# Two-layer diffusion trunk on one core: a written TensorE order for the second layer's experts

## The chip, the cores and the metric

The kernel runs on one core of a Trainium2 chip. The metric is device time in microseconds for one execution; the median of three executions stands for the kernel.

## The reference

The program computes two layers over 256 latent and 256 context tokens of width 1024: attention in four head groups, then a mixture of 16 SwiGLU experts of which each token takes two. The change lies in the experts of the second layer, which are computed for the 256 latent tokens alone:

```python
expert, w = route(hf, router_w, router_b)      # two experts of one group per token, weights sum to 1
xb = hf[buf_t].reshape(n_blocks, MOE_BLOCK, shp[-1])
def expert_block(args):
    xe, e = args
    return (jax.nn.silu(xe @ w_gate[e]) * (xe @ w_up[e])) @ w_down[e]
yb = lax.map(expert_block, (xb, blk_e)).reshape(P, shp[-1])
y = jnp.zeros_like(hf).at[buf_t].add(yb * buf_w[:, None].astype(yb.dtype))
x = x + m_lat[5] * y
```

`w_gate` and `w_up` are 1024 by 512 and `w_down` is 512 by 1024 for each expert, all fp32: six pieces of 1 MB for an expert, 96 for the layer.

## The kernel before

**The stage.** Class `MoeOnChip` computes the second layer's experts, 64 token slots for each. Tokens are neither gathered from nor scattered to DRAM. They are selected and put back by matmuls with 0/1 matrices, and the result is accumulated in four PSUM banks over all 16 experts.

**Names, with the lines of before.** `batch` (from L1253) builds for four experts at a time the 0/1 matrices `OH` on VectorE (L1259) and selects the tokens with them: 32 matmuls in four groups of eight (L1269), each group into one bank called `tr`. ScalarE (L1232) and VectorE (L1230) then bring the bank to `xTb`, each one half of it. `weights` (from L1279) multiplies `OH` with the table `tw` (a token's number and its weight) in eight fp32 matmuls (L1284), which gives each slot its token and weight, `sw`. `first` (from L995) does gate and up of one expert in two halves (L1007); a pair of its matmuls, one for gate and one for up, works on two halves of the array's columns. `hidden` is SiLU (ScalarE L1032), product (VectorE L1033), four transposes (TensorE L1037, bank `tr`) and a copy to `hT` (ScalarE L1046). `second` is w_down, in two halves (L1060, bank `S`). `store` scales the result by weight and gate (VectorE L1311, tile `selm`), splits it in two fp32r parts in `ys` (ScalarE L1314, VectorE L1315), and appends to the list `todo` the four matmuls that add the rows to the four accumulators (`add`, L1320; banks `ada`, `o`, `S`, `tr`).

Since four of the eight banks hold the accumulators, each of the tags `tr` and `S` has one bank left, and `mm` has two.

**Loops.** `experts` (from L1323) goes through e = 0 to 15. Round e issues `first` of expert e+1 with `hidden` of e between its halves, at e = 2, 6 and 10 the `batch` for the next four experts, then the pending `add`, then `second` of e, and at those three rounds `weights`.

**What sets the order.** A scheduler places the instructions of each engine; the code's order is where it starts from, and it may interleave the pieces above. `tc.issue_after` holds an instruction behind another; `tc.keep_in_program_order` keeps the instructions so marked in the order in which the code issues them. Weights come through SyncE's queue (L121) in the order in which they are used, each into a free slot of some 20 of 1 MB; `done_w` frees a slot when its matmuls are done.

Of the kernel before, what the change touches and what calls it, by code (L numbers as in the profile page):

```python
# [25 lines left out]
NE = 16  # L26
# [26 lines left out]
def body(tc, a, dbg=None):  # L53
# [18 lines left out]
    def psum(tag):  # L72
        return ps.tile([128, 512], F32, name=tag, bufs=dict(mm=2, ada=1, tr=2, S=2, o=1)[tag])


# [701 lines left out]

    class Moe:
        def __init__(self, l, tiles, pers, scr):
            self.l, self.tiles, self.scr = l, tiles, scr  # L780
# [215 lines left out]
        def first(self, e, between=None):  # L996
# [32 lines left out]
        def hidden(self, pa, pb):  # L1029
# [6 lines left out]
            for k in range(4):  # L1036
                PE.transpose(pt[:, k], h[:, 128 * k:128 * k + 128], ident[0:64, 0:64])  # L1037
            if pb is not None:
# [10 lines left out]
        def second(self, e):  # L1049
# [3 lines left out]
            for hf in range(2):  # L1053
                wd = next_w(f"e{l}")
                for g in range(2):
                    f = 2 * hf + g
                    for c in range(self.tiles_m):
                        m = 128 // self.tiles_m
                        t, h = c % (64 // m), 512 * (m * c // 64)
                        PE.matmul(py[m * c:m * c + m], lhsT=hT[:, f, m * t:m * t + m], rhs=wd[:, g, h:h + 512],  # L1060
                                  start=f == 0, stop=f == 3)
                if py2 is not None:
# [46 lines left out]
        def next(self, e, p):  # L1109
            def between():  # L1110
                self.hidden(*p)
                self.fetch(e + 2)
            if e + 1 < NE:
                return self.first(e + 1, between)
            self.hidden(*p)

        def overflow(self):
# [87 lines left out]

    class MoeOnChip(Moe):
        def persistent(self, pers):
            self.tw = pers.tile([128, self.nt, NE, 2], F32, name="tw")
            self.ms = pers.tile([128, self.nt, NE], F32, name="ms")
            self.cnt = pers.tile([128, NE], F32, name="cnt")  # L1210
            self.wsum = pers.tile([128, self.nt], F32, name="wsum")
            self.h2s = {}
# [22 lines left out]
        def tables(self, oh, M, pp):  # L1235
            nt, scr, tw = self.nt, self.scr, self.tw
            n16 = 16 * nt
            ms, wsum = self.ms, self.wsum
            for t in range(nt):
                G.tensor_scalar(tw[:, t, :, 0], iot[:, 0:16], 0.0, C["tok"][:, t:t + 1], op0=OP.mult, op1=OP.add)  # L1240

            V.tensor_mul(ms, M, self.score)
            V.tensor_copy(self.cnt, pp[:, n16:n16 + 16])
# [10 lines left out]
        def batch(self, e0):  # L1254
            p2, nt, n = self.p2, self.nt, 4
            OH = []
            for t in range(nt):
# [3 lines left out]
                                op=OP.is_equal)  # L1261
                OH.append(o)
            xT = p2.tile([128, 8, 64 * n], F32, name="xTb")
            for dp in range(4):
                px = psum("tr").rearrange("p (d n) -> p d n", d=2)
                for j in range(2):
                    d = 2 * dp + j
                    for i in range(2 * nt):
                        mm = PE.matmul(px[:, j].rearrange("p (e x) -> p e x", x=64),  # L1269
                                       lhsT=self.h2s[i % nt][i // nt][:, 128 * d:128 * d + 128],  # L1270
                                       rhs=OH[i % nt][:, :, 0], start=i == 0, stop=i == 2 * nt - 1)
# [4 lines left out]
            self.OH, self.last = OH, mm.ins  # L1276
# [26 lines left out]
        def store(self, e, py, py2):  # L1303
# [13 lines left out]
            def add():  # L1317
                for t in range(nt):
                    for c in range(2):
                        PE.matmul(self.acc[t, c], lhsT=oT[:, t], rhs=ys[:, c], start=False, stop=e == NE - 1)  # L1320
            self.todo.append(add)

        def experts(self, p2):  # L1323
            self.p2, self.xt = p2, {}
            self.sw, self.todo = {}, []

            self.sgh, self.y = scr2.rearrange("p a k n -> p (a k n)"), C["sel"].rearrange("p a n -> p (a n)")
            self.batch(0)
# [4 lines left out]
            with tc.issue_after(self.last):  # L1333
                for (t, c), acc in self.acc.items():
                    PE.matmul(acc, lhsT=ident, rhs=X[t][:, 512 * c:512 * c + 512], start=True, stop=False)
            self.rest()
            self.weights(0)
            add_tile("x", xx.rearrange("p t n -> p (t n)"))
            for e in range(NE):
                q = self.next(e, p)  # L1340
                if e % 4 == 2 and e + 2 < NE:
                    self.batch(e + 2)
                while self.todo and q:
                    self.todo.pop(0)()
                self.second(e)
                if e % 4 == 2 and e + 2 < NE:
                    self.weights(e + 2)
                p = q
            while self.todo:
                self.todo.pop(0)()  # L1350

# [15 lines left out]
        def overflow(self):  # L1367
# [3 lines left out]
            with tc.If(v > CAP):  # L1371
                ecol = p2.tile([128, 1], F32, name="ecol")
                V.memset(ecol, 0.0)
                with tc.For_i(0, NE, 1) as ei:
# [5 lines left out]
                    pos = p2.tile([128, nt, 2], F32, name="pos")  # L1380
                    for k, src in enumerate((self.posm, self.tw[:, :, :, 1])):
                        V.tensor_mul(pe_, src, eqb)
                        V.tensor_reduce(pos[:, :, k], pe_, axis=AX.X, op=OP.add)
                    for b in range(-(-(128 * nt - CAP) // 128)):
# [258 lines left out]
```

## Time and profile before

| what | value |
|---|---|
| median of 3 runs | 1273.6 us (1273.07 to 1274.47) |
| the profiled execution's own time | 1278.25 us |
| its span, first to last instruction | 1276.3 us |
| mean granted TensorE clock | 0.961 of full speed |
| busy share of the span: TensorE, VectorE, ScalarE, GpSimd | 91%, 45%, 33%, 19% |

The rows below are of this one execution, and times in them count from the start of its span. The experts of the second layer fill its last fifth, from about 1009 us on. TensorE's weight loads (PEld) overlap its matmuls. An fp32 matmul shows as two instructions, one of fp32r as one.

### The profile page before, as it was taken

The page shows a single profiled execution, that of the slowest core. Times are in us where ns is not written, and L with a number is a line of the kernel's source. Part 1 is how long each engine was busy: PE and PEld are TensorE (multiplying, and loading weights), DVE is VectorE, ACT ScalarE, POOL GpSimd, SP SyncE. Part 2 cuts the span into 40 slices and gives each one's busy share as a digit, 9 for nine tenths or more (in the row PEclk, how much of TensorE's full clock was granted, in tenths as well). Part 3 has the DMA queues.
Part 4 walks back from the last instruction along what each step waited for, and adds up shares of the span by engine and source line. Part 5 has one row for each costly group of instructions (what it writes and reads, how often), then busy time and mean ns, then how long its engine had stood idle before and what let it go on. Part 6 is the DMA issues. An engine that isn't in the chain of part 4 may idle for free.

```text
span 1276.3 us, 21459 instructions
## 1 busy us (share of the span) xinstructions
PE 1161.8 (91%) x8527; PEld 674.5 (53%) x8527; DVE 568.0 (45%) x1539; ACT 417.6 (33%) x1003; POOL 241.9 (19%) x268
## 2 busy tenths in 40 slices
PE   4999999999999589999999957989999699999996
PEld 2676667666645344444444426978875334333332
DVE  4556656565334742132222238785763523222222
ACT  3445445455133311111111115755542312111111
POOL 1231121221112612121121125341311200000000
PEclk9999899999999879999999988998999899999998
DMA  9746445454734569999999754223129799999940
GB/s 300 261 174 232 166 166 187 168 196 137 286 156 175 221 203 353 380 356 369 359 375 378 272 196 163 67 67 109 51 99 353 265 388 394 394 394 394 394 177 34
DMA packets 134639, 312.99 MB, mean 245 GB/s; under 512 B 7212, under 2 KB 38448, under 8 KB 129408
## 3 DMA queue, kind: packets, MB, share of 16 engines
q1 hardware_dynamic: 127936, 294.19, 63.6%
q0 software_dynamic: 3840, 8.40, 2.1%
q10 hardware_dynamic: 2752, 8.91, 1.9%
q8 instruction: 71, 1.16, 0.4%
q14 instruction: 40, 0.33, 0.1%
HBM read 305.11 MB, written 10.55 MB: 247 GB/s over the span
## 4 chain that ended last, share of the span: by engine, by line
PE 59%; DVE 7%; DMA 4%; issue 1%; ACT 1%; POOL 1%; ACTq 0%; SPq 0%; DVEq 0%; POOLq 0%
PE mm L1007 19%; PE S L1060 9%; PE mm L765 5%; PE mm L465 3%; PE o L1012 2%; PE ada L1012 2%; PE S L1066 2%; PE o L712 2%; PE ada L465 2%; PE tr L1269 2%; PE tr L644 1%; PE S L636 1%; PE tr L983 1%; DMA gb<-amd 1%; PE tr L1037 1%
## 5 line engine op out<-in xcount | busy, mean ns | idle before, releaser
L465 PE MATMUL mm<-ws,hT 128*128 128x256 f32 x1488 | 229.9, 296 | 5.4 <-DVE hT L504 1.8
L465 PEld LDWEIGHTS mm<-ws,hT 128*128 128x128 f32 x1488 | 200.8, 195 | 43.1 <-issue 25.1
L1007 PE MATMUL mm<-wb,xT 128*32 128x512 f32 x912 | 141.0, 607 | 0.0
L295 POOL TENSOR_TENSOR hss<-hss,mhalf 128x4 f32<-128x4 f32 (+2 forms) x56 | 66.9, 1196 | 186.6 <-DVE hss L294 170.8
L671 ACT ACTIVATE p<-S,nm 128x512 f32<-128x512 f32 (+1 forms) x120 | 73.7, 616 | 68.4 <-DVE nm L661 41.8
L661 DVE TENSOR_REDUCE nm<-S 128x1 f32<-128x512 f32 (+1 forms) x120 | 70.6, 596 | 26.5 <-PE S L636 22.4
L1060 PE MATMUL S<-wb,hT 128*32 128x512 f32 (+1 forms) x360 | 72.8, 595 | 0.0
L765 PE MATMUL mm<-wa,t4k 128*128 128x512 f32 x144 | 70.9, 615 | 0.0
L1007 PE MATMUL mm<-wb,xTb 128*64 128x512 f32 x240 | 69.6, 623 | 0.0
L974 POOL DMA_INDIRECT yd<-y,idx x32 | 36.9, 1152 | 165.4 <-DVE y L1085 160.6
L314 PE MATMUL ada<-wa,sc 128*32 128x512 f32 x320 | 63.1, 617 | 0.0
L1007 PEld LDWEIGHTS mm<-wb,xT 128*32 128x32 f32 x912 | 34.2, 111 | 49.0 <-issue 44.7
L644 PE MATMUL tr<-ident,p 128*128 128x128 f32 x320 | 51.0, 277 | 4.7 <-ACT p L671 4.4
L1046 ACT ACTIVATE hT<-tr 128x384 f32<-128x384 f32 (+1 forms) x32 | 14.0, 438 | 125.7 <-PE tr L1043 75.1
L452 ACT ACTIVATE ws<-wa 128x512 fp32r<-128x512 f32 x80 | 48.8, 630 | 18.7 <-PE mm L465 7.5
L712 PE MATMUL o<-PT,v 128*64 128x256 f32 x320 | 54.5, 390 | 0.1
L1060 PE MATMUL S<-wa,hT 128*32 128x512 f32 (+1 forms) x312 | 53.2, 593 | 0.6 <-ACT hT L1046 0.6
L454 POOL TENSOR_TENSOR ws<-wa,ws 128x512 fp32r<-128x512 f32 x20 | 27.7, 1387 | 136.5 <-ACT ws L452 110.7
L611 PE MATMUL tr<-identr,sk 128*128 128x128 f32 x312 | 47.6, 254 | 4.8 <-DVE sk L608 2.9
L1007 PE MATMUL mm<-wc,xTb 128*64 128x512 f32 x144 | 52.0, 597 | 0.0
L644 PEld LDWEIGHTS tr<-ident,p 128*128 128x128 f32 x320 | 36.4, 141 | 23.1 <-ACT p L671 11.6
L1033 DVE TENSOR_TENSOR sc<-sc,mm 64x512 f32<-64x512 f32 x16 | 11.0, 690 | 83.8 <-ACT sc L1032 83.7
(319 smaller groups left out, 2043.1 us busy)
## 6 DMA issues: line engine op xcount, KB each, us to landing
wb<-in_w_up_dram SPq DMA_DIRECT2D x49, 1024.0 KB
wa<-in_ada_w_dram SPq DMA_DIRECT2D x48, 1024.0 KB
wb<-in_w_gate_dram SPq DMA_DIRECT2D x38, 1024.0 KB
wb<-in_w_down_dram SPq DMA_DIRECT2D x30, 1024.0 KB
wa<-in_w_down_dram SPq DMA_DIRECT2D x22, 1024.0 KB
wa<-in_w_in_dram SPq DMA_DIRECT2D x20, 1024.0 KB
wc<-in_w_gate_dram SPq DMA_DIRECT2D x11, 1024.0 KB
wa<-in_w_gate_dram SPq DMA_DIRECT2D x10, 1024.0 KB
```

Source lines behind the costliest of these rows:

```text
L295: state["pow"] = G.tensor_tensor(out, x, mhalf[:x.shape[0], :x.shape[1]], op=OP.pow).ins
L314: PE.matmul(pa[32 * c:32 * c + 32], lhsT=sc[:, k], rhs=w[:, 0, 512 * c:512 * c + 512], start=k == 0, stop=k == 7)
L452: S.activation(x[:, 0], r, AF.Copy)
L465: PE.matmul(acc, lhsT=lh[:, k, c], rhs=wp[k // 2][:, rh, k % 2], start=first and k == 0 and i == 0, stop=last and k == 7 and i == 2)
L644: PE.transpose(pt[:, i], p[:, k0 + 128 * i:k0 + 128 * i + 128], ident)
L661: V.tensor_reduce(nm[:, 0:1], s[:, k0:512], axis=AX.X, op=OP.min)
L671: S.activation(p[:, k0:512], s[:, k0:512], AF.Exp, bias=nm_, scale=scale, accum_out=z)
L712: PE.matmul(o[64 * c:64 * c + 64, 256 * j:256 * j + 256], lhsT=v[:, 2 * st + kc, vc:vc + 64], rhs=PTs[c][:, kc], start=kc == 0, stop=kc == ...
L765: PE.matmul(acc, lhsT=self.yT[key][:, t // 2, i, 128 * (t % 2):128 * (t % 2) + 128], rhs=w[key][:, i, 512 * h:512 * h + 512], start=n == 0 ...
L1007: PE.matmul(pa[m * c:m * c + m], lhsT=xT[:, 4 * hk + k, m * t:m * t + m], rhs=w[m * c // 64][:, k], start=hk == 0 and k == 0, stop=hk == 1 ...
L1012: PE.matmul(pb[32 * c:32 * c + 32, 0:256], lhsT=xT[:, 4 * hk + k, 64:96], rhs=w[c // 2][:, k, 256 * (c % 2):256 * (c % 2) + 256], start=hk ...
L1060: PE.matmul(py[m * c:m * c + m], lhsT=hT[:, f, m * t:m * t + m], rhs=wd[:, g, h:h + 512], start=f == 0, stop=f == 3)
```

## The change

1. Every TensorE instruction of `MoeOnChip`'s expert stage is marked to keep the order of the code (`pinned`; `free`, for the first layer, marks nothing).
2. The pending `add` is issued between the halves of `first`, behind the four transposes of `hidden`, as one piece (`rows_back`).
3. `OH` is built a round ahead (`onehot`); `weights` and then `batch` are issued behind `first` and ahead of `second`; the four groups of `batch` go alternately to banks `tr` and `mm`.
4. `weights` takes the weight as a sum of two fp32r parts, in eight fp32r matmuls with four output columns; VectorE adds the two parts. Table `tw` gets a third column, with two more small VectorE operations and one of GpSimd.

```diff
@@ Moe.first, hidden, second: each PE.matmul and PE.transpose is wrapped
-                        PE.matmul(pa[m * c:m * c + m], lhsT=xT[:, 4 * hk + k, m * t:m * t + m], rhs=w[m * c // 64][:, k],
-                                  start=hk == 0 and k == 0, stop=hk == 1 and k == 3)
+                        self.order(PE.matmul(pa[m * c:m * c + m], lhsT=xT[:, 4 * hk + k, m * t:m * t + m],
+                                             rhs=w[m * c // 64][:, k], start=hk == 0 and k == 0, stop=hk == 1 and k == 3))
...
@@ Moe.next
             def between():
                 self.hidden(*p)
                 self.fetch(e + 2)
+                self.rows_back()
...
     class MoeOnChip(Moe):
+        order = staticmethod(pinned)
...
             def rest():
                 V.tensor_reduce(wsum, ms, axis=AX.X, op=OP.add)
                 V.reciprocal(wsum, wsum)
-                V.tensor_mul(tw[:, :, :, 1], ms, wsum.unsqueeze(2).to_broadcast([128, nt, 16]))
-                V.tensor_reduce(self.mx[:, 0:1], self.cnt, axis=AX.X, op=OP.max)
+                V.tensor_mul(ms, ms, wsum.unsqueeze(2).to_broadcast([128, nt, 16]))
+                V.tensor_copy(tw[:, :, :, 1], ms)
+                V.tensor_sub(tw[:, :, :, 2], ms, tw[:, :, :, 1].bitcast(F32))
...
             for dp in range(4):
-                px = psum("tr").rearrange("p (d n) -> p d n", d=2)
+                px = psum(("tr", "mm")[dp % 2]).rearrange("p (d n) -> p d n", d=2)
...
         def weights(self, e0):
             p2, nt, n, OH = self.p2, self.nt, 4, self.OH
             pw = psum("S")
             for e in range(n):
                 for t in range(nt):
-                    PE.matmul(pw[:, 8 * e:8 * e + 2], lhsT=OH[t][:, e].rearrange("p c x -> p (c x)").bitcast(F32),
-                              rhs=self.tw[:, t, e0 + e], start=t == 0, stop=t == nt - 1)
+                    self.order(PE.matmul(pw[:, 8 * e:8 * e + 4], lhsT=OH[t][:, e].rearrange("p c x -> p (c x)"),
+                                         rhs=self.twp[:, t, 3 * (e0 + e):3 * (e0 + e) + 4], start=t == 0, stop=t == nt - 1))
             sw = p2.tile([128, n, 3], F32, name="sw", bufs=2)
-            V.tensor_copy(sw[:, :, 0:2], pw[:, 0:8 * n].rearrange("p (e x) -> p e x", x=8)[:, :, 0:2])
+            pv = pw[:, 0:8 * n].rearrange("p (e x) -> p e x", x=8)
+            V.tensor_copy(sw[:, :, 0:1], pv[:, :, 0:1])
+            V.tensor_reduce(sw[:, :, 1:2], pv[:, :, 1:3], axis=AX.X, op=OP.add)
...
             for e in range(NE):
-                q = self.next(e, p)
-                if e % 4 == 2 and e + 2 < NE:
+                more = e % 4 == 2 and e + 2 < NE
+                if more:
+                    self.onehot(e + 2)
+
+                p = self.next(e, p)
+                if more:
+                    self.weights(e + 2)
                     self.batch(e + 2)
-                while self.todo and q:
-                    self.todo.pop(0)()
                 self.second(e)
-                if e % 4 == 2 and e + 2 < NE:
-                    self.weights(e + 2)
-                p = q
-            while self.todo:
-                self.todo.pop(0)()
+            self.rows_back()
```

**How TensorE's order moves, a plain round.** The lines of the changed kernel are others: L1007 is L1016, L1037 is L1046, L1060 is L1069, L1269 is L1291, L1284 is L1305 and L1320 is L1343. Before, TensorE, from `second` of expert 13 on:

```order
L1060 MATMUL S<-wb_11758,hT 64x512 x4
L1037 MATMUL tr<-ident,sc 128x64 x4
L1060 MATMUL S<-wb_11760,hT 64x512 x4
L1007 MATMUL mm<-wb_11820,xTb 64x512
L1320 MATMUL ada<-ys,oTb 128x512
L1320 MATMUL S<-ys,oTb 128x512
L1320 MATMUL o<-ys,oTb 128x512
L1320 MATMUL tr<-ys,oTb 128x512
L1007 MATMUL mm<-wb_11826,xTb 64x512
```

The changed kernel, TensorE, the same expert; the eight rows of `second` stand ahead of the first half of `first`, whose last three rows begin the piece:

```order
L1016 MATMUL mm<-wb_11842,xTb 64x512
L1016 MATMUL mm<-wb_11836,xTb 64x512
L1016 MATMUL mm<-wb_11842,xTb 64x512
L1046 MATMUL tr<-ident,sc 128x64 x4
L1343 MATMUL ada<-ys,oTb 128x512
L1343 MATMUL o<-ys,oTb 128x512
L1343 MATMUL S<-ys,oTb 128x512
L1343 MATMUL tr<-ys,oTb 128x512
L1016 MATMUL mm<-wb_11862,xTb 64x512
L1016 MATMUL mm<-wb_11864,xTb 64x512
```

The transposes move from inside `second` to between the halves of `first`, and the rows added move from behind the first matmul of `first` (whose partner stood behind them) to behind its eighth.

**A selection.** Before, TensorE, at the round of expert 6, between two of the groups of eight:

```order
L1269 MATMUL tr<-OH_11463,t4k 128x256
L1269 MATMUL tr<-OH_11465,t4k 128x256
L1060 MATMUL S<-wb_11283,hT 64x512 x3
L1269 MATMUL tr<-OH_11463,t4k 128x256
L1269 MATMUL tr<-OH_11465,t4k 128x256
```

The changed kernel, TensorE, at the same round, from the first group to the second:

```order
L1291 MATMUL tr<-OH_11432,t4k 128x256
L1291 MATMUL tr<-OH_11434,t4k 128x256
L1291 MATMUL mm<-OH_11432,t4k 128x256
L1291 MATMUL mm<-OH_11434,t4k 128x256
L1291 MATMUL mm<-OH_11432,t4k 128x256
```

The matmuls of `second` that stood between the groups stand behind the fourth group now, and each group has another bank than the one ahead of it.

## Rows read from the trace of the kernel before

**Rows 1.** Busy time, clock and transfers in 20 us stretches of the experts' stage.

```profile
core 0: us, PE busy (x) PEld busy (x) DVE busy (x) ACT busy (x) POOL busy (x), PEclk, DMA share, GB/s
1020.00:1040.00 20.00, 20.00 (x94) 8.26 (x92) 3.32 (x9) 1.56 (x3) 0.00 (x0) 1.00 0.99 365
...
1240.00:1260.00 20.00, 17.66 (x78) 5.87 (x76) 4.74 (x8) 3.38 (x7) 0.00 (x0) 1.00 0.00 0
```

**Rows 2.** The same view, 200 us of streaming, and where the transfers end.

```profile
1019.40:1219.40 200.00, 189.98 (x870) 75.83 (x868) 51.63 (x101) 34.51 (x62) 0.00 (x0) 0.98 1.03 390
...
1226.00:1228.00 2.00, 2.00 (x10) 0.66 (x9) 0.69 (x1) 0.18 (x1) 0.00 (x0) 1.00 0.34 139
```

**Rows 3.** What TensorE waited for, 1109 to 1265 us: total, times, longest.

```profile
PE ada L1320 <- DVE ys L1315: 7.7, 6, 1.4
PE tr L1269 <- DVE xTb L1230: 2.5, 2, 1.2
PE S L1284 <- DVE selm L1311: 1.7, 2, 0.8
```

**Rows 4.** TensorE in order of time, an early round: start, length, what.

```profile
1080.01 3.65 PE L1060 MATMUL S<-wb,hT 128*64 128x512 f32 x16
1083.49 3.60 PE L1007 MATMUL mm<-wb,xTb 128*64 128x512 f32 x16
1087.02 0.46 PE L1037 MATMUL tr<-ident,sc 64*128 64x64 f32 x4
...
1092.12 3.65 PE L1060 MATMUL S<-wb,hT 128*64 128x512 f32 x16
```

**Rows 5.** The same, a late round; in brackets the idle time ahead and its releaser.

```profile
1224.91 2.30 PE L1060 MATMUL S<-wc,hT 128*64 128x512 f32 x7
...
1229.30 1.02 PE L1007 MATMUL mm<-wc,xTb 128*64 128x512 f32 x2
1231.77 0.50 PE L1320 MATMUL ada<-ys,oTb 128*128 128x512 f32 x1 [1.44 <-DVE ys L1315]
...
1239.64 2.30 PE L1060 MATMUL S<-wb,hT 128*64 128x512 f32 x7
```

**Rows 6.** The same: a selection late in the stage.

```profile
1120.56 1.22 PE L1269 MATMUL tr<-OH,t4k 128*128 128x256 f32 x8 [1.23 <-DVE xTb L1230]
1121.71 1.93 PE L1060 MATMUL S<-wc,hT 128*64 128x512 f32 x6
...
1131.91 5.34 PE L1007 MATMUL mm<-wb,xTb 128*64 128x512 f32 x14
```

**Rows 7.** The same: the first expert's `second`, the last half of the last one's.

```profile
1036.33 3.60 PE L1060 MATMUL S<-wb,hT 128*64 128x512 f32 x16
...
1262.84 1.94 PE L1060 MATMUL S<-wa,hT 128*64 128x512 f32 x8
```

**Rows 8.** The same: the first `weights`.

```profile
1027.10 1.84 PE L1284 MATMUL S<-tw,OH 128*128 128x2 f32 x16
```

**Rows 9.** VectorE and ScalarE in order of time: `store`, `hT`, then one bank of `xTb`.

```profile
1083.71 0.75 DVE L1311 SCALAR_TENSOR_TENSOR selm<-S,sw,gh 128x512 f32<-128x512 f32 x1 [2.80 <-PE S L1060]
1085.22 1.41 DVE L1315 TENSOR_TENSOR ys<-selm,ys 64x512 fp32r<-64x512 f32 x2 [0.76 <-ACT ys L1314]
...
1087.58 0.38 ACT L1046 ACTIVATE hT<-tr 128x256 f32<-128x256 f32 x1 [1.75 <-PE tr L1037]
...
1121.82 0.56 ACT L1232 ACTIVATE xTb<-tr,modT,gs 128x256 f32<-128x256 f32 x1 [1.28 <-PE tr L1269]
...
1122.42 0.55 DVE L1230 TENSOR_SCALAR xTb<-tr,gs,modT 128x256 f32<-128x256 f32 x1 [1.16 <-ACT xTb L1232]
```

**Rows 10.** Stretches as in rows 1: the clock behind a late selection; the first layer's experts.

```profile
1132.00:1134.00 2.00, 2.00 (x6) 0.53 (x8) 1.91 (x5) 0.38 (x1) 0.00 (x0) 0.61 1.05 388
...
540.00:560.00 20.00, 19.96 (x225) 8.77 (x221) 7.54 (x31) 3.06 (x6) 2.98 (x3) 1.00 0.96 355
...
700.00:720.00 20.00, 20.00 (x226) 8.92 (x228) 4.49 (x8) 3.06 (x6) 2.41 (x2) 1.00 1.01 381
```

More of the change, by code (lines that the diff above doesn't have):

```diff
@@ L73, in psum, with pinned, free @@
         return ps.tile([128, 512], F32, name=tag, bufs=dict(mm=2, ada=1, tr=2, S=2, o=1)[tag])
+    def pinned(ins):
+        tc.keep_in_program_order(ins)
+    def free(ins):
+        pass
     def prefer(l, *by):
@@ L778, in body @@
     class Moe:
+        order = staticmethod(free)
         def __init__(self, l, tiles, pers, scr):
@@ L1036, in hidden @@
             for k in range(4):
-                PE.transpose(pt[:, k], h[:, 128 * k:128 * k + 128], ident[0:64, 0:64])
+                self.order(PE.transpose(pt[:, k], h[:, 128 * k:128 * k + 128], ident[0:64, 0:64]))
             if pb is not None:
@@ L1059, in second @@
                         t, h = c % (64 // m), 512 * (m * c // 64)
-                        PE.matmul(py[m * c:m * c + m], lhsT=hT[:, f, m * t:m * t + m], rhs=wd[:, g, h:h + 512],
-                                  start=f == 0, stop=f == 3)
+                        self.order(PE.matmul(py[m * c:m * c + m], lhsT=hT[:, f, m * t:m * t + m], rhs=wd[:, g, h:h + 512],
+                                             start=f == 0, stop=f == 3))
                 if py2 is not None:
@@ L1115, in next, with rows_back @@
             self.hidden(*p)
+        def rows_back(self):
+            pass
         def overflow(self):
@@ L1206, in body @@
     class MoeOnChip(Moe):
+        order = staticmethod(pinned)
         def persistent(self, pers):
[L1208 to L1210 removed]
+            self.twp = pers.tile([128, self.nt, 3 * NE + 1], F32R, name="tw")
+            self.tw = self.twp[:, :, 0:3 * NE].rearrange("p t (e x) -> p t e x", x=3)
             self.wsum = pers.tile([128, self.nt], F32, name="wsum")
@@ L1237, in tables @@
             n16 = 16 * nt
-            ms, wsum = self.ms, self.wsum
+            wsum = self.wsum
             for t in range(nt):
                 G.tensor_scalar(tw[:, t, :, 0], iot[:, 0:16], 0.0, C["tok"][:, t:t + 1], op0=OP.mult, op1=OP.add)
+            G.tensor_copy(self.twp[:, :, 3 * NE:], tw[:, :, 0, 0:1])
+            ms = scr2[:, 0, 0:nt, 0:NE]
             V.tensor_mul(ms, M, self.score)
-            V.tensor_copy(self.cnt, pp[:, n16:n16 + 16])
+            V.tensor_reduce(self.mx[:, 0:1], pp[:, n16:n16 + 16], axis=AX.X, op=OP.max)
             def rest():
@@ L1261, in batch @@
                                 op=OP.is_equal)
-                OH.append(o)
+                self.OH.append(o)
+        def batch(self, e0):
+            p2, nt, n, OH = self.p2, self.nt, 4, self.OH
             xT = p2.tile([128, 8, 64 * n], F32, name="xTb")
             for dp in range(4):
-                px = psum("tr").rearrange("p (d n) -> p d n", d=2)
+                px = psum(("tr", "mm")[dp % 2]).rearrange("p (d n) -> p d n", d=2)
                 for j in range(2):
@@ L1268, in batch @@
                     for i in range(2 * nt):
-                        mm = PE.matmul(px[:, j].rearrange("p (e x) -> p e x", x=64),
-                                       lhsT=self.h2s[i % nt][i // nt][:, 128 * d:128 * d + 128],
-                                       rhs=OH[i % nt][:, :, 0], start=i == 0, stop=i == 2 * nt - 1)
+                        self.order(PE.matmul(px[:, j].rearrange("p (e x) -> p e x", x=64),
+                                             lhsT=self.h2s[i % nt][i // nt][:, 128 * d:128 * d + 128],
+                                             rhs=OH[i % nt][:, :, 0], start=i == 0, stop=i == 2 * nt - 1))
                 for j in range(2):
@@ L1275, in batch @@
                 self.xt[e0 + e] = xT[:, :, 64 * e:64 * e + 64]
-            self.OH, self.last = OH, mm.ins
         def weights(self, e0):
@@ L1319, in add, with rows_back @@
                     for c in range(2):
-                        PE.matmul(self.acc[t, c], lhsT=oT[:, t], rhs=ys[:, c], start=False, stop=e == NE - 1)
+                        self.order(PE.matmul(self.acc[t, c], lhsT=oT[:, t], rhs=ys[:, c], start=False, stop=e == NE - 1))
             self.todo.append(add)
+        def rows_back(self):
+            while self.todo:
+                self.todo.pop(0)()
         def experts(self, p2):
@@ L1327, in experts @@
             self.sgh, self.y = scr2.rearrange("p a k n -> p (a k n)"), C["sel"].rearrange("p a n -> p (a n)")
+            self.onehot(0)
             self.batch(0)
@@ L1332, in experts @@
             self.acc = {(t, c): psum(tags[2 * t + c]) for t in range(2) for c in range(2)}
-            with tc.issue_after(self.last):
-                for (t, c), acc in self.acc.items():
-                    PE.matmul(acc, lhsT=ident, rhs=X[t][:, 512 * c:512 * c + 512], start=True, stop=False)
+            for (t, c), acc in self.acc.items():
+                self.order(PE.matmul(acc, lhsT=ident, rhs=X[t][:, 512 * c:512 * c + 512], start=True, stop=False))
             self.rest()
@@ L1380, in overflow @@
                     pos = p2.tile([128, nt, 2], F32, name="pos")
-                    for k, src in enumerate((self.posm, self.tw[:, :, :, 1])):
-                        V.tensor_mul(pe_, src, eqb)
-                        V.tensor_reduce(pos[:, :, k], pe_, axis=AX.X, op=OP.add)
+                    V.tensor_mul(pe_, self.posm, eqb)
+                    V.tensor_reduce(pos[:, :, 0], pe_, axis=AX.X, op=OP.add)
+                    V.tensor_add(pe_, self.tw[:, :, :, 1].bitcast(F32), self.tw[:, :, :, 2].bitcast(F32))
+                    V.tensor_mul(pe_, pe_, eqb)
+                    V.tensor_reduce(pos[:, :, 1], pe_, axis=AX.X, op=OP.add)
                     for b in range(-(-(128 * nt - CAP) // 128)):
```

4 lines of the change are left out of this document (2 added, 2 removed).

## The prediction, on record before the changed kernel ran

> **What bounds the kernel now.** I read the busy shares by stretches first. In the stage of the experts TensorE is busy nearly all the time, and until shortly before 1227 us so are the transfers [rows 1, 2]. Two resources at 90% and more: which of them sets the end? The transfers deliver 390 GB/s for 200 us and are over at about 1226.7 us (busy 0.34 of the 2 us from 1226 on) [rows 2]. In 1240 to 1260 us nothing is moved, while TensorE works on [rows 1]. The last half of the last `second`, which uses the last load, starts at 1262.84 us [rows 7], 36 us after that load landed. So TensorE is behind its data, and the table of its waits names no transfer [rows 3]: it waits for VectorE, above all at the rows added (L1320, 7.7 us).
>
> Then the order of time. An early round of one expert, from `second` to `second`, takes 1092.12 - 1080.01 = 12.11 us without a gap [rows 4]. A late one takes 1239.64 - 1224.91 = 14.73 us [rows 5] for the same matmuls. 1.44 us of the 2.62 more are the wait for `ys`. The rest comes from broken pairs: the first matmul of `first` stands alone ahead of the rows added, its two instructions take 1.02 us [rows 5], and sixteen of them in pairs take 3.60 us, 0.45 a pair [rows 4]. A late selection has gaps of its own, 1.23 us at one group [rows 6], and behind it the clock falls to 0.61 of full speed, that is to 1.2 GHz for most of the stretch [rows 10].
>
> **The change part by part.** The sum goes over TensorE's path, from the start of the first `second` to the last half of the last one. Before: 1262.84 - 1036.33 = 226.5 us [rows 7].
>
> *Written order and rows added in one piece.* Every round should cost what the early one costs. The rows added now stand behind eight pairs of `first` (1087.02 - 1083.49 = 3.5 us) and the transposes (0.46 us), so `ys` has 4.0 us from the end of `second` [rows 4]. Its chain needs 2.9 us: `selm` starts at 1083.71 us, the second subtraction ends at 1086.63 [rows 9]. The cover is 1.0 us; were it gone, each further microsecond of the chain would cost one in each of 14 rounds. The same four matmuls stand in the early round, only later in it, so 14 rounds at 12.11 us make 169.5 us.
>
> *`weights`.* Sixteen fp32 instructions in 1.84 us [rows 8] become eight of fp32r, with as many columns loaded for each. At the same pace, 0.11 us, they take 0.9 us; at the pace of the fp32r groups in a selection, 1.15 / 8 = 0.14 [rows 6], 1.15 us. I take 0.9, since four moving columns are nearer to two than to 256. VectorE's one more small operation on `sw` lies beside the groups that follow. So do the added operations on the table, long before its first use.
>
> *Selection over two banks.* A group of eight takes 1.15 us (1121.71 - 1120.56) [rows 6]. Emptying its bank takes 0.56 us on ScalarE and then 0.55 us on VectorE, one behind the other, from 1121.82 to 1122.97, so the bank is free about 1.3 us after its group [rows 9]. With two banks in turn the third group waits some 0.2 us and the others nothing: 4 x 1.15 + 0.2 = 4.8 us. With `weights` a selection costs 5.7 us on the path, since nothing of `second` fills it any more. Bounds: no wait at all and a weights part of 0.84, 5.4 us; emptying not covered at all, 4 x (1.15 + 1.3) + 1.15 = 11 us. The two banks make 5.7 the nearer one. Three selections: 17.1 us. The 0/1 matrices are built a round ahead; VectorE has that time.
>
> *The end.* From the last but one `second`: itself 3.5 us, the transposes and `hT` (1087.02 to 1087.96, and a tenth for each handover) 1.1 us, the first half of the last `second` 1.75 us [rows 4, 9]. Together 6.3 us.
>
> *The beginning.* The first `weights` falls by 0.9 us as above, and the lone matmul pair amid the first selection goes, 1.02 against 0.45 us [rows 4, 5]: together 1.5 us ahead of the stretch.
>
> Sum: 169.5 + 17.1 + 6.3 = 192.9 us against 226.5, that is -33.6, and -1.5 for the beginning: **-35.1 us**. The last half of the last `second` then starts at 1262.84 - 35.1 = 1227.7 us. What follows it, 1276.3 - 1262.84 = 13.5 us, stays: the rows of expert 14 are now added behind it, but in the time in which its own `ys` is made.
>
> *What is late next: the transfers.* They streamed without pause already, so they end at 1226.7 us as before, at most 1.5 us sooner, as the first slots come free sooner. The last load is then used only 1.0 us after landing. At 390 GB/s a load of 1.05 MB takes 2.7 us, six of them 16.1 us against TensorE's round of 12.1, so one round further back the reserve is some 4 us larger, and two rounds back 8. TensorE nearly catches up at the very end, and no further gain is left below it: 1226.7 + 13.5 - 1.5 = 1238.7 us of span, a gain of 37.6, is the floor. No transfer is added or moved: SyncE's queue holds the same loads in the same order, and nobody waits longer for a slot.
>
> The profiled execution took 1278.25 us around a span of 1276.3. Taking 35.1 off gives 1243.2 us for such a one. It lies 4.65 us above the median of the runs, which I take off too: 1273.6 - 35.1 = **1238.5 us**.
>
> One rule speaks against the two banks. Behind a late selection the clock stood at 0.61 [rows 10], and 14 matmuls took 5.34 us [rows 6] where pairs at full clock take 14 x 0.225 = 3.15 us; that is 2.2 us a time. The Trainium skill, "TensorE: Matmul & The Clock Gate", section "A second HAM failure mode: psum-queue depth-cycling", tells of a kernel that went from PSUM bank to PSUM bank, paused briefly between groups, and had its clock swing between the two levels. By that rule the fall would stay, or come at all three selections, and the sum would be smaller by up to 7 us. By the rows the fall followed gaps of 1.23 us, which the written order takes away; I take no fall. This is the fourth case below.
>
> **The rivals.**
> 1. *Forecast.* TensorE and the transfers end together; 1235 to 1243 us.
> 2. *The written order waits elsewhere.* `ys` comes late, because VectorE's or ScalarE's queue has something ahead of it, or the banks are not empty in time. For it: the cover is 1.0 us, and the scheduler can no longer put other matmuls in. Against it: in the early round neither engine has more to do than this [rows 9]. One microsecond in 14 rounds costs 14 us, three selections at the upper bound 16 us: about 1253 us at the most, half of it likelier, 1246 us.
> 3. *The transfers are slower.* In the first layer's experts they moved 355 to 381 GB/s [rows 10]. The 80.7 MB from 1019.4 us on (78.0 in 200 us [rows 2], then 7 us more) would take 212 to 227 us, landing at 1231 to 1247 us: 3 to 19 us more, 1242 to 1258 us. Against it: 390 GB/s here, with all engines busy. The Trainium skill, "HBM Reference", section "Specifications (TRN2)", counts about 358 GB/s as one core's share, and about 425 for a core that streams alone. The trace differs from the share; by 358 the time would be 1256 us, by 425 TensorE would set it, as forecast.
> 4. *The clock falls at the selections,* as priced above: 3 x 2.2 us, 1245 us.
> 5. *Slower.* TensorE overtakes its loads early and idles 16.1 - 12.1 = 4 us in each round; the clock then falls to 1.2 GHz and stays there, so that a round takes 24.2 us. It decides from 35.1 / 12.1, three such rounds, on; four give 1273.6 - 35.1 + 48.4 = 1287 us. Against it: four rounds before the end the reserve is still some 16 us, and a half-fast TensorE is soon behind its loads again.
> 6. *Nothing moves.* The program's order does differ at both places shown, so only a loss of the gain's own size would do it.
>
> **How the numbers follow.** Forecast 0.60, the written order's waits 0.15, slower transfers 0.10, the clock 0.08, slower 0.03, nothing 0.02, and 0.02 for a time below 1234. The range 1234 to 1250 us holds the forecast, the fourth case, most of the second and half of the third: some 0.87, so no wider is needed. Within 0.2%, 2.5 us, no difference can be told. Faster by more: 0.95; within: 0.02; slower: 0.03.
>
> **What would show it.** In the profile after: rounds of 12.1 us to the end; no wait for `ys` at the rows added; the selection's 32 matmuls in one piece of 4.6 to 5 us; `weights` at 0.9 to 1.2 us with eight instructions; transfers that end at 1225 to 1227 us, as now, and the last `second` within 3 us of that. The forecast is wrong if TensorE waits in the table for `ys` or a bank by more than some 5 us in all, if transfers end after 1229 us, or if the clock stands below 0.9 in any 20 us stretch between 1040 and 1220 us.

## The result and the profile after

The changed kernel takes 1240.2 us (median of four runs, 1238.48 to 1240.77) against 1274.02 us for the kernel before on the same chip. The ratio is 0.9733, interval 0.972 to 0.9747. The forecast was 1238.5 us.

The profiled execution took 1238.48 us (span 1236.6 us), 1.7 us less than its median, while the one of before lay above its own. So the two spans differ by 39.7 us, and 5.4 of these lie ahead of the stage, where the change only touches small operations on the table: the first selection's matmuls start at 1009.89 us before, at 1004.51 us after. In the profiles of the runs below that keep the work ahead of the stage, this point lies between 1003.95 and 1007.44 us, so a single profile says little there. From there to the last instruction it is 266.4 us before and 232.1 after, **34.3 us less**; 35.1 were forecast.

TensorE of the changed kernel in order of time, a round late in the stage:

```profile
1189.81 3.60 PE L1069 MATMUL S<-wc,hT 128*64 128x512 f32 x16
...
1196.78 0.46 PE L1046 MATMUL tr<-ident,sc 64*128 64x64 f32 x4
1197.16 0.50 PE L1343 MATMUL ada<-ys,oTb 128*128 128x512 f32 x1
...
1201.78 3.60 PE L1069 MATMUL S<-wb,hT 128*64 128x512 f32 x16
```

1201.78 - 1189.81 = 11.97 us, where a late round took 14.73 before [rows 5] and an early one 12.11 [rows 4]. No gap stands ahead of the rows added, and no matmul has lost its partner. The same view at the first of the three later selections:

```profile
1053.55 1.05 PE L1305 MATMUL S<-tw,OH 128*128 128x4 f32 x8
1054.46 1.19 PE L1291 MATMUL tr<-OH,t4k 128*128 128x256 f32 x8
1055.49 1.09 PE L1291 MATMUL mm<-OH,t4k 128*128 128x256 f32 x8
1056.88 1.20 PE L1291 MATMUL tr<-OH,t4k 128*128 128x256 f32 x8 [0.30 <-DVE xTb L1245]
1057.93 1.09 PE L1291 MATMUL mm<-OH,t4k 128*128 128x256 f32 x8
1058.95 3.65 PE L1069 MATMUL S<-wc,hT 128*64 128x512 f32 x16
```

`weights` takes 0.91 us, the four groups 4.49 us with one wait of 0.30. The two others have the same lengths. What TensorE waited for from 1005 us on:

```profile
PE ada L1343 <- DVE ys L1338: 1.5, 1, 1.5
...
PE tr L1291 <- DVE xTb L1245: 0.9, 3, 0.3
PE mm L1016 <- DMA wb<-in_w_up_dram: 0.8, 1, 0.8
...
PE S L1069 <- SPq L1397: 0.5, 1, 0.5
```

Of the 7.7 us for `ys` [rows 3] one wait is left, behind the last `second`, where nothing is left to cover it. New are waits for loads: one is named as such; the one that is put down to SyncE's queue at L1397, the branch ahead of the store of the result, belongs to the last `second`. What it had to wait for is the last load: its packets run out just ahead (below), and the wait is gone in the runs in which the loads are early. Both stand in the order of time at the end:

```profile
1201.78 3.60 PE L1069 MATMUL S<-wb,hT 128*64 128x512 f32 x16
...
1207.07 3.65 PE L1016 MATMUL mm<-wb,xTb 128*64 128x512 f32 x14 [0.84 <-DMA wb<-in_w_up_dram]
...
1215.65 3.98 PE L1069 MATMUL S<-wb,hT 128*64 128x512 f32 x16
1220.57 1.94 PE L1069 MATMUL S<-wd,hT 128*64 128x512 f32 x8 [0.55 <-ACT hT L1055]
1222.95 1.94 PE L1069 MATMUL S<-wa,hT 128*64 128x512 f32 x8 [0.45 <-SPq L1397]
```

The last full round takes 1215.65 - 1201.78 = 13.87 us instead of 11.97, and the end, from there to the last half of the last `second`, 1222.95 - 1215.65 = 7.30. The stretches, with the columns of [rows 1], give the stream and how it ends:

```profile
1019.00:1219.00 200.00, 198.26 (x968) 81.34 (x968) 58.82 (x118) 38.98 (x70) 0.00 (x0) 1.00 1.04 394
...
1222.20:1222.40 0.20, 0.20 (x2) 0.00 (x0) 0.20 (x1) 0.00 (x0) 0.00 (x0) 1.00 0.05 20
1222.40:1222.60 0.20, 0.10 (x2) 0.00 (x0) 0.19 (x1) 0.00 (x0) 0.00 (x0) 1.00 0.00 0
```

394 GB/s for 200 us, with the clock at 1.00 throughout and TensorE busy for 198.26 us of them. The last packets run out at about 1222.4 us, and 0.5 us later the last half of `second` starts. Before, TensorE was some 35 us behind its data, whose last packets came at 1227.6 us or a little later; now the two end together. The same view of before:

```profile
1227.40:1227.60 0.20, 0.20 (x6) 0.13 (x6) 0.00 (x0) 0.00 (x0) 0.00 (x0) 1.00 0.05 20
```

### The profile page after: what moved, and what is told of

Same layout as the page of the kernel before. It is cut to its first block, busy times and chain, and to the rows that moved or that the text cites. A ratio compares the mean times of both kernels' runs of the same rounds, so it can differ in the third digit from the quotient of the medians.

```text
span 1236.6 us, 21407 instructions
## 1 busy us (share of the span) xinstructions
PE 1134.9 (92%) x8495; PEld 667.9 (54%) x8495; DVE 569.3 (46%) x1544; ACT 417.4 (34%) x1003; POOL 242.8 (20%) x269
## 5 line engine op out<-in xcount | busy, mean ns | idle before, releaser
L1016 PE MATMUL mm<-wb,xT 128*32 128x512 f32 x912 | 139.5, 600 | 0.0
L1069 PE MATMUL S<-wb,hT 128*32 128x512 f32 (+1 forms) x360 | 66.5, 593 | 0.0
L1016 PE MATMUL mm<-wb,xTb 128*64 128x512 f32 x240 | 63.2, 596 | 0.8 <-DMA wb<-in_w_up_dram 0.8
L1016 PEld LDWEIGHTS mm<-wb,xT 128*32 128x32 f32 x912 | 34.0, 110 | 47.7 <-issue 43.4
L1069 PE MATMUL S<-wa,hT 128*32 128x512 f32 (+1 forms) x312 | 52.1, 593 | 1.1 <-ACT hT L1055 0.6
L1016 PE MATMUL mm<-wc,xTb 128*64 128x512 f32 x144 | 50.6, 596 | 0.0
L461 DVE TENSOR_TENSOR ws<-wa,ws 128x512 fp32r<-128x512 f32 x60 | 43.5, 738 | 8.7 <-ACT ws L459 8.5
```

The source lines that it names most:

```text
L461: (G if cnt["lo"] % 4 == 0 else V).tensor_sub(x[:, 1], r, x[:, 0].bitcast(F32))
L1016: self.order(PE.matmul(pa[m * c:m * c + m], lhsT=xT[:, 4 * hk + k, m * t:m * t + m], rhs=w[m * c // 64][:, k], start=hk == 0 and k == 0, s ...
L1069: self.order(PE.matmul(py[m * c:m * c + m], lhsT=hT[:, f, m * t:m * t + m], rhs=wd[:, g, h:h + 512], start=f == 0, stop=f == 3))
```

## The experiments

The stretch on which the prediction's sum was made, from the first expert's `second` to the last half of the last one's, is read off each profile in the same way:

| kernel | time, us | ratio to before | stretch, us |
|---|---|---|---|
| before | 1274.02 | 1 | 226.5 |
| changed | 1240.2 | 0.9733 (0.972 to 0.9747) | 193.4 |
| order left to the scheduler | 1257.0 | 0.9866 (0.985 to 0.9883) | 217.3 |
| one bank for the selection | 1256.75 | 0.9854 (0.9826 to 0.9882) | 209.6 |
| `weights` in fp32 | 1240.4 | 0.9744 (0.9727 to 0.9762) | 193.2 |
| rows added behind all of `first` | 1240.66 | 0.9735 (0.9718 to 0.9752) | 194.1 |
| rows not added | 1239.46 | 0.9736 (0.9713 to 0.9758) | 193.5 |
| half of w_down not loaded | 1236.62 | 0.9715 (0.9687 to 0.9743) | 190.6 |
| both of these | 1223.65 | 0.9614 (0.9587 to 0.9642) | 176.9 |
| the written order alone | 1263.35 | 0.9927 (0.9907 to 0.9947) | 214.7 |
| accumulators filled early | 1237.34 | 0.9717 (0.9692 to 0.9743) | 197.4 |
| changed, again | 1239.07 | 0.9724 (0.9699 to 0.9749) | 193.5 |

(Each ratio is to the kernel before as it ran beside the run, 1273.42 to 1274.02 us. In the last row but one the stretch begins earlier, by the time that the filling took; that run is read otherwise, below.) All edits are made to the changed kernel.

### The order left to the scheduler

```diff
     class MoeOnChip(Moe):
-        order = staticmethod(pinned)
+        order = staticmethod(free)
```

> The changed kernel with the marks taken away: the code stands as in the change, but the scheduler places TensorE's instructions of the experts again. In its order the rows added stand once more behind a lone first matmul of the pairs, and the transposes inside w_down, from expert 7 on. Theory A (the written order is what keeps the rounds at 12 us): late rounds of 14.7 us as before, against 11.97 after, some five to seven of them, so 10 to 20 us above the changed kernel, 1250 to 1262 us. Theory B (the places in the code, and the second bank, are enough): within 2 us of the changed kernel, 1238 to 1243 us.

1257.0 us: of the gain of 33.8 us, 16.8 go. TensorE late in the stage:

```profile
1224.82 1.94 PE L1069 MATMUL S<-wb,hT 128*64 128x512 f32 x8
...
1239.55 1.94 PE L1069 MATMUL S<-wb,hT 128*64 128x512 f32 x8
```

14.73 us, the late round of before to the hundredth. An earlier round of the same run shows where:

```profile
1131.55 1.02 PE L1016 MATMUL mm<-wb,xTb 128*64 128x512 f32 x2
1134.02 0.50 PE L1343 MATMUL ada<-ys,oTb 128*128 128x512 f32 x1 [1.44 <-DVE ys L1338]
```

The scheduler again puts one unpaired matmul ahead of the rows added and lets the engine wait 1.44 us, as in [rows 5], although the code now issues the rows behind eight pairs. Issuing them there does not bring the short late rounds; marking the order does.

The other half of the gain, 17.0 us, stays without the marks. From the `second` ahead of a selection to the next but one it takes 29.1, 33.6 and 34.4 us here, against 31.6, 37.9 and 39.1 before. And the scheduler does one thing that the marks forbid: it moves a part of the accumulators' filling (L1362) ahead of the first selection, so that it is 22.2 us from there to the first `second` instead of 25.0. So the marks are worth more in the stretch, 23.8 us between these two profiles, than the 16.8 us of the times. (The profiled execution of this run, 1260.0 us, lies 3.0 us above its median.)

### One bank for the selection

```diff
-                px = psum(("tr", "mm")[dp % 2]).rearrange("p (d n) -> p d n", d=2)
+                px = psum("tr").rearrange("p (d n) -> p d n", d=2)
```

> The changed kernel with all four groups of a selection in bank tr. Theory A (TensorE's path counts in full): each group but the first waits for its bank to be emptied, about 1.3 us, three times in each of the three late selections, against 0.3 us once now: 3 x 3.6 = 11 us more, less up to 2 us in which TensorE waits for loads now: 1249 to 1252 us. Theory B (the transfers set the end): at most 4 us more, below 1245 us. Theory C (pauses at a bank bring the clock down): A's waits, and behind each selection a stretch at 1.2 GHz, 2 us each: 1253 to 1260 us with a granted clock below 0.95 in stretches around 1057, 1114 and 1171 us.

1256.75 us, above what the waits alone would cost. (The four runs are 1251.11, 1256.47, 1257.03 and 1257.36 us, at nearly the same mean clock; the lowest would fit the waits alone, and only the one of 1256.47 has a profile.) TensorE at the first of the three selections, and the clock in the stretches around it:

```profile
1055.69 1.05 PE L1305 MATMUL S<-tw,OH 128*128 128x4 f32 x8
1056.60 1.19 PE L1291 MATMUL tr<-OH,t4k 128*128 128x256 f32 x8
1059.02 1.21 PE L1291 MATMUL tr<-OH,t4k 128*128 128x256 f32 x8 [1.24 <-DVE xTb L1245]
1061.47 2.08 PE L1291 MATMUL tr<-OH,t4k 128*128 128x256 f32 x8 [1.24 <-DVE xTb L1245]
1064.78 2.08 PE L1291 MATMUL tr<-OH,t4k 128*128 128x256 f32 x8 [1.24 <-DVE xTb L1245]
1066.79 4.31 PE L1069 MATMUL S<-wc,hT 128*64 128x512 f32 x16
```

```profile
1058.00:1060.00 2.00, 0.98 (x8) 0.98 (x8) 0.54 (x1) 0.39 (x1) 0.00 (x0) 1.00 1.03 388
...
1062.00:1064.00 2.00, 1.54 (x8) 1.25 (x6) 0.00 (x0) 0.42 (x1) 0.00 (x0) 0.50 1.05 388
...
1066.00:1068.00 2.00, 2.00 (x9) 1.09 (x9) 1.32 (x3) 0.56 (x1) 0.00 (x0) 0.50 1.04 382
```

The selection with `weights` takes 11.1 us instead of 5.4. Three waits of 1.24 us are 3.4 us more than the single one of 0.30. Nearly all of the rest is the clock, at 0.50 (1.2 GHz) from the third group on: two groups of 2.08 instead of some 1.1 us each, and a `second` of 4.1 instead of 3.5, some 2.9 us in all. Together 6.3 us a time, 19.0 for three. 16.2 appear in the stretch, since the 2.9 us in which the changed kernel waits for loads (below) go. At the other two selections (11.5 and 10.2 us) the fall comes at the second and at the fourth group.

This is the fourth rival, on the kernel that it fits. The Trainium skill, "TensorE: Matmul & The Clock Gate", section "A second HAM failure mode: psum-queue depth-cycling", tells of a clock that swings where TensorE goes through PSUM banks and idles briefly between groups. Here the change of bank is harmless: four groups over two banks, with one pause of 0.30 us, stay at 1.00. With one bank and pauses of 1.24 us the clock falls. Of what that section describes, it is the pauses that matter here, though they alone do not say when the fall comes (last section).

### `weights` in fp32

```diff
-                    self.order(PE.matmul(pw[:, 8 * e:8 * e + 4], lhsT=OH[t][:, e].rearrange("p c x -> p (c x)"),
-                                         rhs=self.twp[:, t, 3 * (e0 + e):3 * (e0 + e) + 4], start=t == 0, stop=t == nt - 1))
+                    self.order(PE.matmul(pw[:, 8 * e:8 * e + 4], lhsT=OH[t][:, e].rearrange("p c x -> p (c x)").bitcast(F32),
+                                         rhs=self.twp[:, t, 3 * (e0 + e):3 * (e0 + e) + 4].bitcast(F32), start=t == 0, stop=t == nt - 1))
```

> The changed kernel with the slot weights multiplied in fp32, not in fp32r parts (the same instructions, read as fp32). Theory A (TensorE's path): four times 1.75 us instead of 0.9 to 1.0 us, so 3 us more, less what the end absorbs in its waits for loads: 1241 to 1244 us. Theory B (the transfers set the end): no difference, 1239.5 to 1241 us.

1240.4 us, no difference that can be measured. TensorE at the end:

```profile
1205.38 3.60 PE L1069 MATMUL S<-wb,hT 128*64 128x512 f32 x16
1217.35 3.60 PE L1069 MATMUL S<-wb,hT 128*64 128x512 f32 x16
...
1223.64 1.89 PE L1069 MATMUL S<-wa,hT 128*64 128x512 f32 x8
```

The last round takes 11.97 us and the last half starts without a wait: every wait for a load is gone. TensorE has 3 x 0.9 us more to do, and yet the stretch is 0.3 us shorter; it also begins 1.2 us later, counted from the first selection's first matmul, since the first `weights` is longer too. The fp32r parts do save 0.9 us a time, and give it back at the end.

### The rows added behind all of `first`

```diff
                 self.hidden(*p)
                 self.fetch(e + 2)
-                self.rows_back()
...
+                if e + 1 < NE:
+                    self.rows_back()
                 self.second(e)
```

> The changed kernel with the rows added issued behind the whole of gate and up, ahead of w_down, in the written order, where the early rounds of the kernel before had them. Theory A (what counts is that pairs stay whole and ys is ready; the place itself does not): within 1.5 us of the changed kernel, 1238.5 to 1242 us. Theory B (the place between the halves is what pays): rounds of more than 12 us, 2 us and more above the changed kernel.

1240.66 us. The rounds are 12.11 us here, those of [rows 4], which have the rows at this place: between the halves of `first` they cost 0.14 us less. The rounds with a selection go the other way (17.34 us instead of 17.47), so that TensorE has some 1.1 us more to do in all. The stretch is 0.6 us longer, the rest is taken up by shorter waits for loads. What counts is a place with cover, not which.

### Rows not added, half of w_down not loaded, and both

```diff
-            self.todo.append(add)
+            if e == NE - 1:
+                self.todo.append(add)
```

```diff
-            stream(tv, src.rearrange("(k p) n -> p k n", p=128))
+            sv = src.rearrange("(k p) n -> p k n", p=128)
...
+            if nm == "e1" and view == 1024 and state["down"] > 8:
+                nc.gpsimd.memset(tv[:, 1:2], 0.0)
+                stream(tv[:, 0:1], sv[:, 0:1])
+            else:
+                stream(tv, sv)
```

> The changed kernel without the rows added, for all experts but the last: 60 of the 64 matmuls that add rows are left out, so the output is not the reference's. Theory A (TensorE and the transfers meet at the end): TensorE saves 15 x 1.05 us, but then waits for the loads, which end as now: 1 to 3 us less, 1237 to 1239 us, with waits of 10 us and more for loads in the table. Theory B (TensorE alone sets the end): 14 us less, 1226 us.

> The changed kernel with only half of each w_down piece loaded from the fifth expert on; the other half is set to zero by the idle GpSimd, so the output is not the reference's. 12.6 MB less to move, 32 us at 394 GB/s; TensorE's work is unchanged. Theory A (they meet at the end): only TensorE's 2 us of waits for loads go, 1237 to 1239 us. Theory B (the transfers set the end, TensorE has room): 5 us less and more, below 1235 us.

> The two before this one together: no rows added but the last expert's, and half of each w_down piece from the fifth expert on; the output is not the reference's. Theory A (each of the two hides the other): both gains appear together, 15 x 1.05 + 2 = 18 us less, 1221 to 1225 us. Theory B (something else, VectorE's chain or the slots, sets the rounds): well above that, 1230 us and more.

Less work for TensorE alone: 1239.46 us, nothing gained that can be measured. What its table of waits gained instead:

```profile
PE mm L1016 <- DMA wb<-in_w_up_dram: 2.4, 3, 1.6
...
PE mm L1016 <- DMA wa<-in_w_up_dram: 1.6, 1, 1.6
PE mm L1016 <- DMA x<-in_w_up_dram: 1.6, 1, 1.6
```

With the shorter ones the waits for loads make 8.0 us, less than the 10 that were expected. As much again is lost around them: gate matmuls run without their partner, whose load is late, and behind the last of the long waits the clock is at 0.50 for some 3 us (14 matmuls take 5.34 us there).

Fewer loads alone: 1236.62 us, 3.6 below the changed kernel, though its runs (1234.92 to 1240.51 us) overlap with that one's. The transfers are over at about 1193 us, some 30 us earlier, and TensorE goes on as before:

```profile
1194.00:1196.00 2.00, 2.00 (x12) 0.67 (x10) 0.55 (x1) 0.00 (x0) 0.00 (x0) 1.00 0.00 0
```

```profile
1203.77 3.60 PE L1076 MATMUL S<-wb,hT 128*64 128x512 f32 x16
...
1215.73 3.60 PE L1076 MATMUL S<-wb,hT 128*64 128x512 f32 x16
...
1222.02 1.89 PE L1076 MATMUL S<-wa,hT 128*64 128x512 f32 x8
```

Its stretch of 190.6 us is what TensorE needs when no load is late; the changed kernel's 193.4 holds 2.9 us of waiting, 1.90 in the last round and 1.01 in the end. Both together: 1223.65 us, 16.5 less, where the single edits brought 0.7 and 3.6. Each hides the other. That is what two resources that end together look like, and it settles the forecast's main statement.

### The written order alone

The order marked, but with one bank and fp32 `weights`, and at the places they had: the selection ahead of the rows added, these ahead of `second`, `weights` behind it. To the edits of the one bank and of fp32 `weights`, and without the call of `rows_back` between the halves, come these:

```diff
                 p = self.next(e, p)
                 if more:
-                    self.weights(e + 2)
                     self.batch(e + 2)
+                if e + 1 < NE:
+                    self.rows_back()
                 self.second(e)
+                if more:
+                    self.weights(e + 2)
```

> The written order alone: TensorE keeps the order of the code of the kernel before (a selection in one bank, ahead of the rows added, which come ahead of w_down; the slot weights in fp32, behind w_down). Theory A (the parts add up): plain rounds of 12 us, selections as in the run with one bank (11 us more), weights as in the run in fp32 (3 us more): 1251 to 1256 us. Theory B (the order alone brings it all): 1239 to 1244 us. Theory C (without a scheduler to fill the gaps the selections cost more than they did before): 1260 us and more.

1263.35 us: the order alone brings 10.2 of the 33.8 us. The rounds are 12.11 us, so its gain is there and at the end; the selections give some of it back:

```profile
1055.07 1.21 PE L1290 MATMUL tr<-OH,t4k 128*128 128x256 f32 x8
1057.52 1.21 PE L1290 MATMUL tr<-OH,t4k 128*128 128x256 f32 x8 [1.24 <-DVE xTb L1244]
...
1063.45 0.40 PE L1342 MATMUL ada<-ys,oTb 128*128 128x512 f32 x1
...
1068.98 1.95 PE L1304 MATMUL S<-tw,OH 128*128 128x4 f32 x16 [0.85 <-DVE selm L1333]
```

```profile
1070.00:1072.00 2.00, 2.00 (x13) 1.28 (x14) 1.22 (x2) 0.30 (x1) 0.00 (x0) 0.83 1.03 412
1072.00:1074.00 2.00, 2.00 (x8) 0.57 (x6) 1.75 (x6) 0.00 (x0) 0.00 (x0) 0.50 1.01 399
```

Per selection 8.38 us for the groups instead of 4.49, 0.85 of waiting for `selm`, 1.0 more for `weights`, and some 1.8 in the first half of `first` behind it, at 0.50: 7.5 us, 22.4 for three. With 14 rounds at 0.14 us more that is 24.4 us above the 190.6 that TensorE needs; the stretch shows 24.2. The scheduler of before had filled such gaps with matmuls of `second` [rows 6], all of them in the first of the three selections, some in the others: from the `second` ahead of a selection to the next but one it takes 37.2 us here each time, against 31.6, 37.9 and 39.1 before. In the order as written nothing stands in these gaps, and it is the second bank that takes them away.

The parts do not add up: 17.0 us without the marks, 10.2 by the order alone, 33.8 together. The order shows in full only together with the second bank; the fp32r parts and the place of the rows added change nothing that can be measured (above).

### The accumulators filled early, and the changed kernel again

The profile showed where both resources lose time together: ahead of the stage. TensorE waits 6 us for the routing, the clock falls, and the loads pause for some 10 us, because all slots are full until the first matmuls of `first`.

```diff
+            self.accumulators()
             pp = psum("S")
...
-            tags = ["ada", "o", "S", "tr"]
-            self.acc = {(t, c): psum(tags[2 * t + c]) for t in range(2) for c in range(2)}
-            for (t, c), acc in self.acc.items():
-                self.order(PE.matmul(acc, lhsT=ident, rhs=X[t][:, 512 * c:512 * c + 512], start=True, stop=False))
```

(The removed lines are the body of `accumulators`, which `route` now calls ahead of the routing's matmuls.)

> The changed kernel, with the four accumulators filled (L1362, eight matmuls of the residual with a unit matrix, 1017.64 to 1020.8 us) while TensorE waits for the routing (996.5 to 1003.2 us, 6.08 us in one wait) instead of between the first expert's gate and up and its second half. Nothing else moves. Theory A (the transfers set the end): loads pause from about 1006 to 1015 us, since every slot is full until the first matmuls of gate and up have used theirs, and the end follows from when they resume. The filling lies behind that point, so its 3.2 us are hidden; only what starts the first matmul of gate and up sooner counts. If the granted clock, 0.50 from 996 to 1009 us, stays higher through the filling, the first selection falls from 6.1 us to as little as 4.5: the time is 1.0 to 2.0 us below the changed kernel beside it, and none if the clock falls all the same. TensorE then keeps about 3 us of reserve, and its waits for loads in the last two rounds grow by that. Rival B (TensorE sets the end): 3.2 us and the clock's share come off, 1235 to 1237 us.

> The changed kernel once more, unedited, beside the run with the accumulators filled early on the same chip. Theory A and rival B alike: 1240.2 us within 1.5, since its four runs so far lay between 1238.5 and 1240.8 us. A difference above 2 us would say that chips or calls differ by as much as the effects disputed here, and that only kernels of one call can be compared that closely.

1237.34 us (1236.73 to 1242.17) beside 1239.07 us (1237.23 to 1241.29): 1.7 us apart, within what the intervals leave open. Only the profiles tell more. First the edited kernel, then the changed one of the same call, each with the stretch from 1006 us on behind it:

```profile
1008.97 0.38 PE L1301 MATMUL tr<-OH,t4k 128*128 128x256 f32 x1 [1.01 <-DVE OH L1287]
...
1014.01 7.09 PE L1020 MATMUL mm<-wc,xTb 128*64 128x512 f32 x32
```

```profile
1006.00:1008.00 2.00, 1.17 (x8) 0.34 (x6) 1.70 (x11) 0.00 (x0) 0.00 (x0) 1.00 1.04 381
```

```profile
1005.90 2.46 PE L1291 MATMUL tr<-OH,t4k 128*128 128x256 f32 x8 [1.01 <-DVE OH L1277]
1008.17 1.91 PE L1291 MATMUL mm<-OH,t4k 128*128 128x256 f32 x8
...
1013.01 7.09 PE L1016 MATMUL mm<-wc,xTb 128*64 128x512 f32 x32
```

```profile
1006.00:1008.00 2.00, 1.98 (x8) 1.69 (x9) 1.34 (x7) 0.00 (x0) 0.00 (x0) 0.50 0.41 150
```

The first selection takes 5.0 us instead of 7.1, since the clock is back at 1.00 by 1006 us. From its start to the last half of the last `second` it is 217.9 us instead of 219.5. But the changed kernel's first profile has 218.4 there, with 6.1 us for the first selection, so most of these 1.6 us is what executions of one kernel differ by. Counted from the first matmul of `first`, with which slots begin to come free for the loads, the last half of the last `second` starts 212.3 us later in the changed kernel, 212.4 in its repetition, 212.4 without the rows added and 212.9 with the filling moved, although the last two have some 14 and 3.2 us less for TensorE to do in that time. So the end follows the loads, as theory A has it; the filling only moved work into the wait for the routing. Whether this version is faster than the changed kernel is not shown.

## Why the prediction was right, step by step

- **The bound.** Right: TensorE was the bound, some 35 us behind its data, and the gain ended where the transfers do.
- **Rounds.** 14 x 12.11 us were forecast, 11.97 measured: 2.0 us less in all. The early round of [rows 4] has the rows added at another place than the changed kernel, and the new place is a little cheaper.
- **The cover for `ys`.** Forecast 1.0 us, though its own rows give 0.8, since `selm` starts 0.2 us behind w_down. 0.8 it is in the changed kernel (the last subtraction ends at 1196.36 us, the rows added start at 1197.16), and it held in every round, with no wait until the last. The second rival (1246 to 1253 us) did not come about, but the run with the order left to the scheduler shows that its opposite, a free order, does cost such a wait.
- **Selection.** 5.7 us forecast, 5.4 measured: `weights` 0.91 as taken, the third group's wait 0.30 (0.2 forecast), the groups 1.05 apart instead of 1.15. The upper bound for one bank, 11 us, was 11.1 in the run, but for a reason that the bound did not have: the waits make only 3.4 us of the 5.7 more, the clock nearly all of the rest.
- **The end.** 6.3 us forecast; 6.29 where no load is late, 7.30 in the changed kernel. **The beginning.** -1.5 forecast; the first selection to the first `second` takes 25.0 us against 26.44, -1.4.
- **The sum.** 192.9 us forecast, 193.4 measured, but two errors cancel in it, which is luck. TensorE's own work is 190.6 us, 2.3 less than forecast; waiting for loads, put at nothing, is 2.9.
- **The step that failed in size: the transfers' end.** It was set at 1226.7 us from the mean share of a 2 us stretch [rows 2], with 1.0 us of reserve and a floor 2.5 us below the forecast. But a load thins out: its last packets, at a share of 0.05, run 0.4 us past the bulk, and TensorE starts 0.5 us behind the last one. Before, they had done the same, until a microsecond behind 1226.7 us. In time from the first selection's matmul, the last packet comes at 217.9 us in the changed kernel and at 217.7 or a little later before, so nothing came sooner either. There was no reserve; the forecast was the floor.
- **Slower transfers.** No: 394 GB/s with all engines busy. The Trainium skill, "HBM Reference", section "Specifications (TRN2)", counts about 358 GB/s as one core's share and about 425 for a core alone. The trace lies between, and nearer to the core alone.
- **The clock.** As taken, no fall with two banks; with one bank the rival would have come, at 2.9 us in the selection shown where 2.2 were forecast.
- **Slower, nothing moves.** Neither of them: TensorE catches up with its loads only at 1207 us, so it never idles for long.

## What to carry to other kernels

A written order pays where a scheduler breaks a good pattern, but it also takes away what the scheduler filled gaps with: give each place that had a gap its own cover, here a second bank, before fixing the order. When a resource stops being the bound, look for the next one at the same end: here both end within 1 us, so further edits on either alone (fp32r parts, cheaper places, fewer loads) bring nearly nothing, and only both together show. Read the end of a stream packet by packet, not from a mean share.

## What the runs showed of the hardware that was not expected

- The same three pauses of 1.24 us brought the granted clock to 0.50 at the third, the second and the fourth group in the three selections of one run. In the run with the order alone it stayed at 1.00 through all four groups, and fell at 1071 us, in dense work 2 us behind a further wait of 0.85 us (for `selm`). When it falls can't be read off the pauses alone; what decides was not tried.
- What stands next to a matmul counts: the same four matmuls of the rows added cost 0.14 us a round less behind the transposes (rounds of 11.97 us) than behind `first` (12.11).
